# Expert outputs summed in PSUM by group of experts, with gathered residual rows and scattered output rows

## Chip, core and metric

The kernel runs on one core of one Trainium2 chip. The metric is the device time of one execution in microseconds. Time before: median 813.35 us of three runs (811.8 to 814.05).

## What is computed

One encoder layer of 512 tokens with 1024 features: latent attention and pooling, cross attention, a hierarchical mixture of experts, a last norm. The change touches the last two. The group router picks one of 4 groups for each token, then 2 of the group's 8 experts:

```python
group_prob = softmax(xn @ w_rg + b_rg)            # 4 groups
g_w, g_idx = top_k(group_prob, 1)
e_logits = (xn @ w_re + b_re).reshape(B, S, 4, 8)
sel = e_logits of the chosen group
e_w, e_idx = top_k(softmax(sel), 2); e_w = e_w / sum(e_w)
cw[token, expert] = g_w * e_w
out = 0
for e in range(32):
    hid = silu(xn @ w_gate[e]) * (xn @ w_up[e])   # 1024 -> 256
    out = out + (hid * cw[..., e:e+1]) @ w_down[e]
h = h + out
return rms_norm(h, final_norm_g)
```

Both experts of a token lie in one group, so all that the mixture adds to a token comes from 8 consecutive experts.

## The kernel before

Up to `finish_dense` the dense layers run; their instructions are the same in both kernels except for a few small tables of the router. `finish_dense` transposes the residual stream to rows, writes the rows with their 1/rms to the DRAM scratch H3 (512 x 1025) and calls `router`. `router` gives each expert 64 slots and makes `src`, the token of each slot. An empty slot's index is out of bounds, so that its row isn't moved.

`experts` takes the 32 experts as 16 pairs of two, side by side in the columns of TensorE's array. Each expert has three pieces of weights of 1 MB: two of gate and up, one of down. `e_load` issues them on SP's queue in the order of use, into 18 slots of 1 MB (and two places that are used once), so that 20 of the 96 pieces come ahead of the loop; `e_done` hands a slot back when the last product that reads its piece has been issued. The last pair's two pieces of down come in eight quarters. For a pair p the loop does: `up(p)`, 16 products over 8 feature tiles (L1492), then silu on ScalarE (L1502) and the product with up on VectorE (L1503), and the gather of the rows of pair p+3 (L1456, GpSimd); `take(p+1)`, 8 transposes of the next pair's gathered rows (L1474); `turn(p)`, 2 transposes of the hidden rows (L1522); `down(p)`, 8 products (L1538), whose result is scaled by the slot's weight `cws` and split in two float32r halves Y, high by ScalarE (L229) and low by VectorE (L230).

`add(p, i, n)` brings the pair's rows back to the order of the tokens: the one-hot table OH (slots x 512 tokens, by GpSimd in `places`, L1516) times the two halves of Y (L1554), for token tile i and half n of the features, so 8 times two products for each pair, and VectorE adds each bank onto the residual stream in SBUF (L1556). The 8 are queued in `steps`: four run inside the next pair's `up`, one after every second feature tile, two before `turn`, two after it.

The slots' weights `cws` come by memory: `weights` computes two per token, SP writes them to the DRAM scratch CW (L1573), and GpSimd gathers one column for each pair (`weights_of`, L1462). After the last pair, `run` works off the list TAIL: the last adds, squares (L1641), 1/rms (L1644 to L1651), scaling (L1659) and 8 output DMAs of 256 KB (L1661).

Of the kernel before, what the change touches and what calls it, by code (L numbers as in the profile page):

```python
# [6 lines left out]
F32 = mybir.dt.float32  # L7
# [16 lines left out]
# columns of the stacked gains  # L24
# [30 lines left out]
class Arena:  # L55
# [6 lines left out]
    def alloc(self, n, long=False):  # L62
        """the next place after the last one, or for a long time at the top of a gap"""
# [24 lines left out]
    def take(self, at, n):  # L88
        self.used.append((at, at + n))
        self.used.sort()  # L90
        self.peak = max(self.peak, sum(b - a for a, b in self.used))
# [16 lines left out]
class Buf:  # L108
    """A piece of an arena: `ap` is [128, n]; `f` reads it as float32."""
# [33 lines left out]
class Kernel:  # L143
# [8 lines left out]
    TAIL = "a00 p01 | q00 a01 q01 a10 q10 p11 a11 s00 q11 a20 s01 q20 p21 s11 a21 a30 q21 p31 q30 a31 q31 s10 s20 s21 s30 s31"  # L152
    ACT_SCALE = ()
# [60 lines left out]
    # ---- small things  # L214
# [3 lines left out]
    def split(self, src, dst, scale=None, hi_eng="act"):  # L218
        """dst.hi = round(src*scale), dst.lo = src*scale - dst.hi; APs."""
# [23 lines left out]
    # ---- the stream of the dense weights  # L243
# [27 lines left out]
    def w_need(self, upto, ahead=0):  # L271
        """split the weights of the stream up to and with item `upto`, and some more if there is room"""
# [48 lines left out]
    def bcast(self, col, nt, dst):  # L321
        """dst[p, t] = col of token t, for all p"""
# [7 lines left out]
    # =====================================================================  # L330
# [14 lines left out]
    def start(self):  # L345
        nc, a = self.nc, self.a
        # loads
# [22 lines left out]
        # while the first loads come  # L370
# [6 lines left out]
        # constants  # L377
        jp = self.jp = self.const([128, 128], I32, "jp")
        nc.gpsimd.iota(jp, pattern=[[1, 128]], base=0, channel_multiplier=-1)
        self.ident = self.const([128, 128], F32, "ident")  # L380
        nc.vector.tensor_scalar(self.ident, jp, 0.0, None, op0=ALU.is_equal)
        self.ones = {}
# [11 lines left out]
        # x * g in two parts; sums of squares; the first five output tiles  # L394
# [43 lines left out]
        # rotary tables: rows of 32: cos, +-sin, cos, +-sin  # L438
# [11 lines left out]
        # the rotary key, the first pool channels  # L450
# [8 lines left out]
        # latents: kv (2 tiles) and q (3 tiles), raw times their gains, in two parts, and squares  # L459
# [18 lines left out]
        # r1 along the tokens  # L478
# [6 lines left out]
        for n, sc in (("kv", 1.0), ("q", 96.0)):  # L485
# [4 lines left out]
            # (m r1^2 + eps)^-1/2 * r1 (* 1/sqrt(96))  # L490
# [10 lines left out]
        # rotate: rows cos-part, sin-part, twice  # L501
# [32 lines left out]
    def pool_u(self, g, b=None):  # L534
        """pool channels: u, trailing means by doubling"""
# [33 lines left out]
    def mid(self):  # L569
# [18 lines left out]
        # pooled channels  # L588
# [22 lines left out]
        # c_kv along the tokens  # L611
# [9 lines left out]
    def keys(self, j, b):  # L621
        """two heads: rows nope | rope | rope and rope | rope | nope"""
# [10 lines left out]
    def key_rows(self):  # L633
        """the rotary rows are the same for all heads"""
# [7 lines left out]
    def values(self):  # L642
        """values: [keys, head, hi 64 | lo 64]"""
# [25 lines left out]
    # ---- chunk-causal attention, head by head; the first gate's tiles fill the tensor engine  # L669
    def attention(self):  # L670
# [134 lines left out]
        # the last head; the first tiles of the projection of the others  # L805
# [30 lines left out]
    def mix(self):  # L836
        nc, a = self.nc, self.a
        atk = self.atk
        # the residual stream again
# [113 lines left out]
    def cross(self):  # L953
# [3 lines left out]
        # keys [dim, mem]  # L957
# [31 lines left out]
        # values [mem, dim]; the first queries before the last of them  # L989
# [20 lines left out]
        # queries' rstd / sqrt(256)  # L1010
# [93 lines left out]
    # ---- the last projection, the router's logits, the rows for the experts  # L1104
    def finish_dense(self):
# [5 lines left out]
        # rows of the scratch: the residual stream and, in the last column, rstd  # L1111
# [9 lines left out]
        # router weights, hi | lo  # L1121
# [3 lines left out]
        # the last tile's logits come from its float32 rows: the gain goes into the weights  # L1125
# [68 lines left out]
        # (mean of squares + eps)**-0.5: the last tile's part comes alone  # L1194
# [19 lines left out]
        # the logits as rows  # L1214
# [15 lines left out]
    def tmp(self, shape, name, dt=F32):  # L1230
        """a small tile of the arena, freed by tmp_free"""
# [10 lines left out]
    def router_consts(self):  # L1242
# [6 lines left out]
        i32([128, 8], "itile", [[1, 8]], -8, 0)  # L1249
        i32([128, 1], "ipart", [[0, 1]], 0, 1)  # L1250
        self.tri = self.tmp([128, 128], "tri", BF16)
# [3 lines left out]
        # two identities on top of each other: the sum of the parts of the logits  # L1255
# [5 lines left out]
        self.rhs = [self.tmp([128, 4, 3, NE], f"rhs{k}", BF16) for k in range(2)]  # L1261

    def router(self, b):
# [11 lines left out]
        # the group: first maximum; the logits of the experts come meanwhile  # L1275
# [18 lines left out]
        # its experts: the first two maxima, with the others' logits out of reach  # L1294
# [9 lines left out]
        for k in range(2):  # L1304
            nc.vector.tensor_tensor(out=A[k], in0=self.iota64[:, None, :NE].to_broadcast([128, 4, NE]),
                                    in1=I8[:, :, k:k + 1].to_broadcast([128, 4, NE]), op=ALU.is_equal)
            # what the slots shall know of their tokens: its place in the tile, the tile and choice, the tile
            nc.scalar.activation(self.rhs[k][:, :, 0], A[k], AF.Copy, scale=self.ipart)

        def tiles(k, eng):  # L1310
            for v, o in ((1, 4 * k), (2, 4)):
                eng.tensor_tensor(out=self.rhs[k][:, :, v], in0=A[k],
                                  in1=self.itile[:, o:o + 4, None].to_broadcast([128, 4, NE]), op=ALU.mult)
# [15 lines left out]
        # while the ranks come  # L1329
# [6 lines left out]
        self.put(b)  # L1336
# [5 lines left out]
        b = self.bank()  # L1342
        z = self.banks[b][:, :48]
# [5 lines left out]
        z = z.rearrange("p (q e) -> p q e", q=3)  # L1349
# [3 lines left out]
        self.dst = self.const([128, 16], I32, "dst")  # L1353
        nc.vector.tensor_scalar(t1, z[:, 0], 512.0, None, op0=ALU.add)
        nc.vector.scalar_tensor_tensor(out=self.src, in0=z[:, 2], scalar=128.0, in1=t1, op0=ALU.mult, op1=ALU.add)
        nc.vector.tensor_scalar(t1, t1, 512.0, None, op0=ALU.add)
        nc.vector.scalar_tensor_tensor(out=self.dst, in0=z[:, 1], scalar=128.0, in1=t1, op0=ALU.mult, op1=ALU.add)
        self.put(b)
        # the fullest expert
        self.over = self.const([128, 1], I32, "over")  # L1360
        nc.vector.tensor_reduce(out=self.over, in_=cnt, op=ALU.max, axis=AX.X)
        self.put(b2)
        # weights: p(group) / (1 + exp(l2 - l1)) and the rest of it
        w = self.cw = [self.const([128, 4], F32, f"w{k}") for k in range(2)]
        d = c([128, 4], "d21")

        def weights():
            nc.vector.tensor_tensor(out=ge, in0=lg, in1=gm[:, :, None].to_broadcast([128, 4, 4]), op=ALU.subtract)
# [486 lines left out]
```

## Time and profile before

| | |
|---|---|
| median of the runs shown | 813.35 us |
| the profiled execution: span of its trace | 810.7 us |
| its own time outside the trace | not given; the median lies 2.65 us over the span |
| TensorE busy (matmul) | 769.2 us, 95% |
| VectorE, ScalarE, GpSimd busy | 455.1, 303.6, 166.2 us |
| moved by DMA | 157.66 MB |
| TensorE busy, 560 to 780 us | all of it |

The span ends with the last instruction of the slowest engine. A busy TensorE in these pages is a modelled end of each product; the distance between the starts of products is the safer clock. In the rows "idle before <-releaser" names what ended a wait. SPq is SP's queue of DMA issues.

### The profile page before, as it was taken

The numbers are of one execution on the slowest core, as the hardware profiler recorded it, in microseconds if no ns is written. First come the engines' busy times: TensorE is split into PE (matmuls) and PEld (weight loads), VectorE is DVE, ScalarE is ACT, GpSimd is POOL, SyncE is SP. The second block draws the span as 40 slices with busy tenths as digits, with TensorE's granted clock in tenths as the row PEclk, the third lists the DMA queues.
The fourth block names the chain that finished last, engine by engine and source line by source line (L and its number), as shares of the span: only waits on it lengthen the run. The fifth ranks groups of instructions, "written<-read, shape, count | busy, mean of one in ns | idle before, by whom it ended". The sixth has DMA issues, their size and how long they took to land.

```text
span 810.7 us, 10122 instructions
## 1 busy us (share of the span) xinstructions
PE 769.2 (95%) x3714; PEld 522.8 (64%) x3714; DVE 455.1 (56%) x812; ACT 303.6 (37%) x572; POOL 166.2 (21%) x196
## 2 busy tenths in 40 slices
PE   8999999999999989999999998469999999999995
PEld 6877788878786868999888886223344334433342
DVE  6847444777786848874555545114455444544454
ACT  7443323665565625543443443111122211221123
POOL 4245101021111424300001012135312111212002
PEclk9999999999999989999999999599999999999998
DMA  9311323202220733475511999988999999999103
GB/s 329 106 59 29 115 86 123 82 17 72 66 65 27 230 107 85 142 193 153 189 53 29 384 300 278 188 207 323 388 393 401 394 395 387 404 394 412 67 1 106
DMA packets 44868, 157.66 MB, mean 194 GB/s; under 512 B 7568, under 2 KB 17424, under 8 KB 33296
## 3 DMA queue, kind: packets, MB, share of 16 engines
q1 hardware_dynamic: 40992, 149.33, 53.9%
q0 software_dynamic: 3104, 6.31, 2.1%
q10 hardware_dynamic: 720, 1.35, 0.5%
q8 instruction: 30, 0.49, 0.3%
q14 instruction: 22, 0.18, 0.1%
HBM read 156.97 MB, written 4.20 MB: 199 GB/s over the span
## 4 chain that ended last, share of the span: by engine, by line
PE 78%; DVE 6%; DMA 5%; issue 5%; ACT 3%; POOL 3%; SPq 0%; POOLq 0%; DVEq 0%; ACTq 0%
PE b L235 14%; PE b L1492 14%; PE b L236 13%; PE b L237 13%; PE b L1554 8%; PE b L1538 7%; PE b L1474 2%; DMA CW<-w 1%; DMA R<-in_we 1%; PE b L700 1%; PE b L745 1%; DMA F<-in_wd 1%; PE b L702 1%; DVE R L227 1%; PE b L701 1%
## 5 line engine op out<-in xcount | busy, mean ns | idle before, releaser
L1556 DVE TENSOR_TENSOR F<-b,F 128x512 f32<-128x512 f32 x124 | 81.3, 686 | 98.0 <-PE b L1554 98.0
L1554 PE MATMUL b<-B 128*128 128x512 f32 x248 | 81.9, 433 | 5.4 <-ACT B L229 5.4
L1554 PEld LDWEIGHTS b<-B 128*128 128x128 f32 x248 | 40.0, 189 | 58.8 <-issue 49.3
L1502 ACT ACTIVATE F<-b,F 128x256 f32<-128x256 f32 x16 | 7.6, 474 | 135.8 <-PE b L1492 126.1
L1456 POOL DMA_INDIRECT F<-H,src x16 | 17.1, 1066 | 157.6 <-DVE F L1503 143.8
L230 DVE SCALAR_TENSOR_TENSOR B<-b,cws,B 128x512 fp32r<-128x512 f32 x32 | 23.9, 750 | 41.7 <-ACT B L229 41.7
L229 ACT ACTIVATE B<-b,cws 128x512 fp32r<-128x512 f32 x32 | 21.9, 687 | 62.7 <-PE b L1538 52.0
L237 PE MATMUL b<-H,R 128*128 128x512 f32 x108 | 42.8, 397 | 0.0
L1492 PE MATMUL b<-W,F 128*64 128x512 f32 x80 | 38.4, 602 | 0.0
L411 PE MATMUL b<-H,Q 128*128 128x512 f32 x120 | 27.8, 392 | 1.4 <-ACT Q L224 1.4
L1474 PE MATMUL b<-ident,F 128*128 128x128 f32 x128 | 17.6, 283 | 10.5 <-DMA F<-H,src 10.5
L720 ACT ACTIVATE F<-b,sm,cc_q 128x128 f32<-128x128 f32 (+3 forms) x32 | 19.8, 618 | 19.0 <-DVE sm L719 17.4
L411 PEld LDWEIGHTS b<-H,Q 128*128 128x128 f32 x120 | 22.4, 188 | 6.9 <-ACT Q L224 2.3
L235 PE MATMUL b<-H,G 128*128 128x512 f32 x60 | 25.0, 417 | 1.3 <-ACT H L224 1.3
L227 DVE TENSOR_TENSOR R<-W,R 128x1024 fp32r<-128x1024 f32 (+2 forms) x17 | 22.8, 1345 | 5.5 <-ACT R L224 4.8
L1516 POOL TENSOR_SCALAR B<-F,srcf 128x512 fp32r<-128x512 f32 x16 | 25.3, 1586 | 0.5
L1474 PEld LDWEIGHTS b<-ident,F 128*128 128x128 f32 x128 | 15.5, 146 | 14.1 <-DMA F<-H,src 11.4
L236 PE MATMUL b<-H,G 128*128 128x512 f32 x60 | 23.7, 394 | 0.7 <-DVE H L227 0.7
L237 PEld LDWEIGHTS b<-H,R 128*128 128x128 f32 x108 | 20.6, 190 | 4.5
L224 ACT ACTIVATE E<-W 128x1024 fp32r<-128x1024 f32 (+3 forms) x24 | 18.9, 797 | 10.9 <-PE b L236 3.6
L1538 PE MATMUL b<-H,F 128*64 128x512 f32 x96 | 21.9, 599 | 0.8 <-ACT F L1525 0.8
L1479 ACT ACTIVATE F<-b,gcol 128x128 f32<-128x128 f32 x60 | 17.1, 368 | 14.1 <-PE b L1474 14.1
(574 smaller groups left out, 2141.0 us busy)
## 6 DMA issues: line engine op xcount, KB each, us to landing
W<-in_wd SPq DMA_DIRECT2D x62, 512.0 KB, 3.7
H<-in_we SPq DMA_DIRECT2D x20, 1024.0 KB, 8.4
F<-in_we SPq DMA_DIRECT2D x13, 1024.0 KB, 9.9
Q<-in_we SPq DMA_DIRECT2D x12, 1024.0 KB, 7.7
R<-in_we SPq DMA_DIRECT2D x12, 1024.0 KB, 7.6
W<-in_we SPq DMA_DIRECT2D x10, 1024.0 KB, 8.4
E<-in_we SPq DMA_DIRECT2D x5, 1024.0 KB, 8.7
G<-in_we SPq DMA_DIRECT2D x5, 1024.0 KB, 7.8
```

The costliest lines, as they stand in the source:

```text
L227: nc.vector.tensor_tensor(out=lo, in0=src, in1=hi.bitcast(F32), op=ALU.subtract)
L230: nc.vector.scalar_tensor_tensor(out=lo, in0=src, scalar=scale, in1=hi.bitcast(F32), op0=ALU.mult, op1=ALU.subtract)
L235: nc.tensor.matmul(out, l[0], r[0], start=start, stop=False)
L236: nc.tensor.matmul(out, l[0], r[1], start=False, stop=False)
L237: nc.tensor.matmul(out, l[1], r[0], start=False, stop=stop)
L411: nc.tensor.matmul(self.banks[banks[m]], w[l], x[r], start=k == 0 and l + r == 0, stop=k == 7 and l == 1)
L1474: nc.tensor.transpose(self.banks[b][:, k * 128:(k + 1) * 128], x[:, f:f + 128], self.ident)
L1492: nc.tensor.matmul(self.banks[b][r], x[:, k, r], self.e_get(e, k // 4).ap[:, s], start=k == 0, stop=k == 7)
L1516: nc.gpsimd.tensor_scalar(OH[p].ap, self.iotat.ap, self.srcf[:, p:p + 1], None, op0=ALU.is_equal)
L1538: nc.tensor.matmul(self.banks[b][r], h.ap[:, k * 128 + 64 * i:k * 128 + 64 * i + 64], self.e_get(e, 2).ap[:, s], start=k == 0, stop=k == 1)
L1554: nc.tensor.matmul(self.banks[b], OH[p].ap[:, i * 128:(i + 1) * 128], y.ap[:, ns], start=j == 0, stop=j == 1)
L1556: nc.vector.tensor_add(h, self.banks[b].rearrange("p (m f) -> p m f", m=4), h)
```

## The change

- `add` goes by groups. The 4 pairs of a group write into 4 banks (2 tiles of 128 group slots x 2 halves of the features) that stay open over the 4 pairs; 4 times two products for each pair instead of 8 times two, and no add on VectorE. The one-hot table has 256 columns (a token's rank in its group) in place of 512. The adds leave `up`: half of them stand before `turn`, half behind it.
- After a group's last pair, `sums` (VectorE adds of the 4 banks to the residual rows HG, squares on ScalarE), `output` (scaling, and two indirect DMAs on GpSimd that scatter the rows to `out`). `residual` gathers the group's rows of H3 into HG by two indirect DMAs. For the last group the residual goes into the banks by products with the identity, and scaling reads the banks.
- `weights` runs ahead of `take(0)` and is longer. `lists`, behind `up(0)`, makes the slots' ranks and weights (`zs`) and the group's tokens (`gsrc`) by 24 small products. CW, its two writes and the 16 gathers of weights are gone.

```diff
-            for v, o in ((1, 4 * k), (2, 4)):
-                eng.tensor_tensor(out=self.rhs[k][:, :, v], in0=A[k], ...
+            eng.tensor_tensor(out=self.rhs[k][:, :, 1], in0=A[k],
+                              in1=self.itile[:, :, None].to_broadcast([128, 4, NE]), op=ALU.mult)
...
         def weights():
+            for k in range(2):
+                nc.gpsimd.tensor_copy(cb[:, k, :, 0], v)
...
+            nc.vector.tensor_copy(cb[:, :, :, 1], w)
+            for k in range(2):
+                nc.vector.tensor_tensor(out=rhs2[k], in0=A[k][:, :, None, :].to_broadcast([128, 4, 4, NE]),
+                                        in1=cb[:, k, :, :, None].to_broadcast([128, 4, 4, NE]), op=ALU.mult)
+            nc.vector.tensor_tensor(out=JG, in0=self.iotag[:, None, :].to_broadcast([128, 4, 256]),
+                                    in1=v[:, :, None].to_broadcast([128, 4, 256]), op=ALU.is_equal)
+        def lists():
+            for par in range(2):
+                for n in range(8):
+                    nc.tensor.matmul(z[64 * par:64 * par + 64], J[k][:, i], rhs2[k][:, i, :, par::2], ...)
+            nc.scalar.activation(zs, z.rearrange("p (q e) -> p q e", q=4), AF.Copy)
+            for t in range(2):
+                for i in range(4):
+                    nc.tensor.matmul(z[:, 8 * t:8 * t + 8], JG[:, i, t * 128:(t + 1) * 128], rhs3[:, i], ...)
...
-                if k % 2:
-                    step(1)
...
-        def add(p, i, n):
-            b = self.bank()
-                nc.tensor.matmul(self.banks[b], OH[p].ap[:, i * 128:(i + 1) * 128], y.ap[:, ns], start=j == 0, stop=j == 1)
-            nc.vector.tensor_add(h, self.banks[b].rearrange("p (m f) -> p m f", m=4), h)
+        def add(p, n):
+            for t in range(2):
+                if p % PG == 0:
+                    acc[t, n] = self.bank()
+                for j, y in enumerate((Y[p].hi, Y[p].lo)):
+                    nc.tensor.matmul(self.banks[acc[t, n]], OH[p].ap[:, t * 128:(t + 1) * 128], y.ap[:, n * 512:(n + 1) * 512],
+                                     start=p % PG == 0 and j == 0, stop=p % PG == PG - 1 and j == 1)
...
-        weights_of(0)
...
+            if p:
+                add(p - 1, 0)
             turn(p)
-            step(2)
-            if p < NP - 1:
-                down(p)
-                steps += [lambda i=i, n=n, p=p: add(p, i, n) for n in range(2) for i in range(4)]
+            if p:
+                add(p - 1, 1)
+            if p and p % PG == 0:
+                sums()
...
+            down(p)
+            if p and p % PG == 0:
+                output(p // PG - 1)
+            if p % PG == 1:
+                residual(p // PG)
```

TensorE's order from one pair's `up` to the next. Before, with L1492 the products of `up`, L1554 those of `add`, L1474 and L1522 the transposes, L1538 `down`:

```order
L1492 MATMUL b_84<-H,F 64x512 x4
L1554 MATMUL b_83<-B 128x512 x2
L1492 MATMUL b_84<-H,F 64x512 x4
L1554 MATMUL b_78<-B 128x512 x2
L1492 MATMUL b_84<-Q,F 64x512 x4
L1554 MATMUL b_81<-B 128x512 x2
L1492 MATMUL b_84<-Q,F 64x512 x4
L1554 MATMUL b_85<-B 128x512 x2
L1474 MATMUL b_82<-ident,F 128x128 x4
L1474 MATMUL b_80<-ident,F 128x128 x4
L1554 MATMUL b_79<-B 128x512 x2
L1554 MATMUL b_83<-B 128x512 x2
```

Of the changed kernel the same stretch with the rest of the pair (L1540 `up`, L1522 and L1564 the transposes, L1598 `add`, L1580 `down` of the pair):

```order
L1540 MATMUL b_80<-H,F 64x512 x8
L1540 MATMUL b_80<-Q,F 64x512 x8
L1522 MATMUL b_83<-ident,F 128x128 x4
L1522 MATMUL b_82<-ident,F 128x128 x4
L1598 MATMUL b_78<-B 128x512 x2
L1598 MATMUL b_84<-B 128x512 x2
L1564 MATMUL b_79<-ident,F 128x128 x2
L1598 MATMUL b_81<-B 128x512 x2
L1598 MATMUL b_85<-B 128x512 x2
```

The four interruptions of `up` are gone; the adds around `turn` stay as many as they were.

VectorE's order at the start of the experts. Before, `take(0)` (L1481) comes first and the weights (L1368 to L1375) behind it:

```order
L1361 TENSOR_REDUCE over<-b_84 128x1
L1481 TENSOR_SCALAR B<-b_80,gcol 128x128 x4
L1368 TENSOR_TENSOR F<-F 128x16
L1369 TENSOR_TENSOR F<-F 128x4
L1372 TENSOR_REDUCE F<-F 128x4
```

In the changed kernel (L1394 to L1404 are the end of `weights`, L1529 is `take(0)`):

```order
L1394 CAST F<-w 128x8
L1395 TENSOR_TENSOR F<-w,F 128x8
L1396 CAST F<-F 128x8
L1397 TENSOR_TENSOR F<-F 128x8
L1399 TENSOR_TENSOR B<-A_3762,F 128x512
L1399 TENSOR_TENSOR B<-A_3763,F 128x512
L1401 TENSOR_TENSOR B<-iotag,F 128x1024
L1403 TENSOR_SCALAR F<-F 128x4x4
L1404 SCALAR_TENSOR_TENSOR F<-F 128x4x4
L1529 TENSOR_SCALAR B<-b_80,gcol 128x128 x4
```

The two L1399 wait for GpSimd's copies (`cb`), which stand on GpSimd behind the first gathers and two loads; `take(0)` now stands behind all of it.

## Rows read from the trace of the kernel before

**Rows 1.** The page: span, and the span in 40 slices of 20.3 us.

```profile
span 810.7 us, 10122 instructions
...
PE   8999999999999989999999998469999999999995
...
PEclk9999999999999989999999999599999999999998
DMA  9311323202220733475511999988999999999103
```

**Rows 2.** Timeline of TensorE over one pair: start, length, line, tiles, count; the trace counts each float32 product twice.

```profile
645.22 1.89 PE L1492 MATMUL b<-H,F 128*64 128x512 f32 x8
647.03 0.74 PE L1554 MATMUL b<-B 128*128 128x512 f32 x2
...
649.56 0.73 PE L1554 MATMUL b<-B 128*128 128x512 f32 x2
...
654.62 0.73 PE L1554 MATMUL b<-B 128*128 128x512 f32 x2
...
655.98 1.18 PE L1554 MATMUL b<-B 128*128 128x512 f32 x4
...
657.13 1.17 PE L1554 MATMUL b<-B 128*128 128x512 f32 x4
658.23 0.64 PE L1538 MATMUL b<-Q,F 128*64 128x512 f32 x1
...
661.71 0.59 PE L1492 MATMUL b<-G,F 128*64 128x512 f32 x1
```

**Rows 3.** Waits of SP's queue from 540 us on: who waited for whom, us in total, times, longest.

```profile
SPq L1427 <- PE b L1492: 98.0, 24, 11.1
SPq L1427 <- PE b L1538: 74.2, 14, 6.4
```

**Rows 4.** DMA in one pair's time, 644.79 to 661.30 us: packets; then queue, packets, MB, share of the 16 engines (q0 is GpSimd's gathers).

```profile
DMA packets 1012, 6.58 MB, mean 398 GB/s; under 512 B 181, under 2 KB 181, under 8 KB 239
...
q1 hardware_dynamic: 870, 6.32, 95.0%
q0 software_dynamic: 141, 0.24, 3.8%
```

**Rows 5.** Windows: length, busy time of PE, PEld, DVE, ACT, POOL, then granted clock, DMA share, GB/s.

```profile
540.00:560.00 20.00, 14.62 (x56) 6.05 (x56) 7.09 (x14) 3.26 (x8) 13.40 (x12) 0.83 0.91 357
683.00:723.00 40.00, 40.00 (x183) 16.87 (x182) 19.16 (x37) 7.96 (x20) 5.62 (x5) 1.00 0.99 394
723.00:752.00 29.00, 29.00 (x129) 11.27 (x129) 14.00 (x26) 5.53 (x13) 8.16 (x6) 1.00 1.02 411
760.00:780.00 20.00, 20.00 (x92) 7.87 (x88) 9.78 (x18) 4.06 (x9) 0.00 (x0) 1.00 0.00 0
```

**Rows 6.** Timeline of the start of the experts, several engines, in brackets the wait and its releaser.

```profile
506.06 0.74 DVE L1340 TENSOR_TENSOR F<-F 128x256 bf16<-128x256 f32 x2
...
521.17 0.58 POOL L1427 DMA_DIRECT2D C<-in_we  x1
...
522.33 1.97 PE L1474 MATMUL b<-ident,F 128*128 128x128 f32 x8 [10.46 <-DMA F<-H,src]
523.56 1.12 DVE L1481 TENSOR_SCALAR B<-b,gcol 128x128 f32<-128x128 f32 x4 [15.05 <-PE b L1474]
...
506.52 0.97 PE L1347 MATMUL b<-F 128*64 128x48 bf16 x16 [1.23 <-DVE F L1340]
...
534.93 3.65 PE L1538 MATMUL b<-H,F 128*64 128x512 f32 x16 [0.83 <-ACT F L1525]
...
538.61 1.08 POOL L1462 DMA_INDIRECT cws<-CW,dst  x1 [13.12 <-DMA CW<-w]
...
545.68 1.49 PE L1554 MATMUL b<-B 128*128 128x512 f32 x2 [5.38 <-ACT B L229]
```

**Rows 7.** The chain of work that ended last: the piece on the writes of CW (start, us, what).

```profile
526.95 10.88 DMA CW<-w
```

**Rows 8.** The end: timelines of single engines, then the time from issue to landing of the gathers of rows and of the output DMAs.

```profile
789.82 3.65 PE L1538 MATMUL b<-H,F 128*64 128x512 f32 x16
...
793.55 0.69 ACT L229 ACTIVATE B<-b,cws 128x512 fp32r<-128x512 f32 x1 [1.03 <-PE b L1538]
...
793.97 1.02 PE L1626 MATMUL b<-F,ident 128*128 128x512 f32 x2
...
794.78 0.74 DVE L230 SCALAR_TENSOR_TENSOR B<-b,cws,B 128x512 fp32r<-128x512 f32 x1
...
798.00 0.58 ACT L1641 ACTIVATE F<-b 128x512 f32<-128x512 f32 x1
...
803.21 0.27 POOL L1647 TENSOR_SCALAR ms<-ss,ms 128x1 f32<-128x1 f32 x1
803.56 0.55 POOL L1651 TENSOR_TENSOR rs<-ms,expo 128x1 f32<-128x1 f32 x1
...
804.81 0.75 DVE L1659 SCALAR_TENSOR_TENSOR F<-b,rs,F 128x512 f32<-128x512 f32 x1
...
DMA to landing us min/median/max: 4.3/8.4/9.5
...
DMA to landing us min/median/max: 2.3/2.5/3.4
```

More of the change, by code (lines that the diff above doesn't have):

```diff
@@ L1526, in turn, with down @@
             self.put(b)
[L1528 removed]
+        def down(p, between=lambda n: None):
             es = (2 * p, 2 * p + 1)
@@ new lines, in experts, with residual, rows, square @@
+        ms, rs = self.const([128, 2], F32, "ms"), self.const([128, 2], F32, "rs")
+        def residual(g):
+            for t in range(2):
+                nc.gpsimd.indirect_dma_start(
+                    out=HG[t].ap[:, :1025], out_offset=None, in_=self.H3,
+                    in_offset=bass.IndirectOffsetOnAxis(ap=self.gsrc[:, t, g:g + 1], axis=0),
+                    bounds_check=511, oob_is_err=False)
+        def rows(t, n):
+            return HG[t].ap[:, n * 512:(n + 1) * 512]
+        def square(t, n, src):
+            nc.scalar.activation(junk.ap, src, AF.Square, accum_out=ss[n][:, t:t + 1])
+            c = slice(t, t + 1)
+            nc.gpsimd.tensor_scalar(ms[:, c], ss[n][:, c], 1.0 / D, ms[:, c] if n else EPS, op0=ALU.mult, op1=ALU.add)
+            if n:
+                nc.gpsimd.tensor_tensor(out=rs[:, c], in0=ms[:, c], in1=self.expo[:, :1], op=ALU.pow)
@@ L1561, in experts, with sums, output @@
+        def sums():
+            for t in range(2):
+                for n in range(2):
+                    b = acc.pop((t, n))
+                    nc.vector.tensor_add(rows(t, n), self.banks[b], rows(t, n))
+                    self.put(b)
+                    square(t, n, rows(t, n))
+        def output(g):
+            for t in range(2):
+                for n in range(2):
+                    scale(t, n, rows(t, n))
+                scatter(g, t)
         self.e_slots(self.WA)
@@ L1592, in experts @@
                 self.BA = self.seg("B", F32R)
-                XS[0] = self.F(1024)
+                self.hT.free()
+                at = lambda n, o: Buf(self.FA, n, at=o)
+                XS[0] = at(1024, 0)
+                XS.append(at(1024, 1024))
+                self.gl = at(1024, 2048)
                 self.xg_row()
                 gather(2)
-                places(0)
+                HG = [self.F(1025, long=True) for _ in range(2)]
+                for v in HG:
+                    nc.gpsimd.memset(v.ap, 0.0)
@@ L1624, in preload @@
-        def preload(i, n):
-            b = pre[i, n] = self.bank()
-            nc.tensor.matmul(self.banks[b], self.ident, rows[i, n], start=True, stop=False)
-        def last(i, n):
-            if (i, n) not in pre:
-                add(P, i, n)
-                return
-            b = pre[i, n]
-            for j, y in enumerate((Y[P].hi, Y[P].lo)):
-                nc.tensor.matmul(self.banks[b], OH[P].ap[:, i * 128:(i + 1) * 128], y.ap[:, n * 512:(n + 1) * 512],
-                                 start=False, stop=j == 1)
@@ L1663, in run @@
-        def run(order):
-            for op in order.split():
-                i, n = int(op[1]), int(op[2])
-                if op[0] == "p":
-                    preload(i, n)
-                elif op[0] == "a":
-                    last(i, n)
-                elif op[0] == "q":
-                    square(i, n)
-                    done.add((i, n))
-                    if (i, 1 - n) in done:
-                        rstd(i)
-                else:
-                    scale(i, n)
-        done = set()
@@ L1679, in experts @@
-        first, rest = self.TAIL.split("|")
-        down(P, lambda: run(first))
-        run(rest)
-        for b in pre.values():
+            if p:
+                add(p - 1, 1)
+            if p and p % PG == 0:
+                sums()
+            if p == NP - 1:
+                for n in range(2):
+                    for t in range(2):
+                        nc.tensor.matmul(self.banks[acc[t, n]], self.ident, rows(t, n), start=False, stop=False)
+                break
+            down(p)
@@ L1683, in experts, with last @@
+            if p and p % PG == 0:
+                output(p // PG - 1)
+            if p % PG == 1:
+                residual(p // PG)
+        P = NP - 1
+        def last(n):
+            add(P, n)
+            for t in range(2):
+                square(t, n, self.banks[acc[t, n]])
+        down(P, last)
+        for t in range(2):
+            for n in range(2):
+                scale(t, n, self.banks[acc[t, n]])
+            scatter(3, t)
+        for b in acc.values():
             self.put(b)
-        Y.pop(P).free(), OH.pop(P).free()
```

182 lines of the change are left out of this document (86 added, 96 removed).

## The prediction

> **What bounds the kernel now.** First the page in slices [rows 1]: from the 28th slice on (some 547 us) TensorE is full and so are the DMA engines, at 9 of 10, until the weights are all in; in the last slices TensorE works alone. The experts' stage thus has two limits that lie close together, and the prediction turns on how close. The timeline of one pair shows the first [rows 2]: from one `up` to the next 661.71 - 645.22 = 16.49 us, with no idle time on TensorE. The four adds inside `up` start at 647.03, 649.56, ... 654.62, that is every 2.53 us. Eight products of `up` come between two of them; at the pace of `down`, 16 products in 3.65 us less the last one's tail, some 0.215 us each, these are 1.72 us. So one interruption takes 0.81 us: two products of 0.215 us and 0.38 us for the two changes of shape.
>
> The second limit is in the DMA view of the same pair [rows 4]: 6.58 MB in 16.51 us, the hardware queue at 95.0% and GpSimd's gathers at 3.8% of the engines' time. The engines are busy nearly all of it. SP's queue does wait for slots, 172 us in all [rows 3], so the loads are paced by TensorE, but by a TensorE that is hardly slower than the DMA. The windows give 394 GB/s for 683 to 723 us, and 411 at the end of the loads, where the queue is deepest [rows 5]. After 752 us nothing is loaded (760 to 780: 0 GB/s), and TensorE needs 41 us more to its last `down` at 793.5 [rows 8]: that is the stock of loaded pieces, some 2.5 pairs.
>
> **Part by part. Adds out of `up`:** four interruptions of 0.81 us a pair, 3.24 us; TensorE's pair falls from 16.49 to 13.25 us. The adds around `turn` stay the same in number and place, so the cover of silu and of ScalarE's copy stays. A pair's OH and Y are ready one pair earlier, so no new wait. VectorE loses 8 adds a pair and had idle time already: no effect on the end. GpSimd's `places` halves in width: nothing, it was covered.
>
> **What the loads then allow.** From the end of `down(0)` on, 96 - 22 = 74 pieces are still to come (20 ahead of the loop, 2 after `up(0)`): 74 x 1.049 = 77.6 MB. Gathers of 12 pairs at 0.24 MB [rows 4] add 2.9, the residual rows 512 x 4.1 KB = 2.1, the scattered rows of three groups 1.6 MB: 84.2 MB. At 411 GB/s that is 205 us, 16.6 us a pair's worth with the new traffic, and TensorE wants one in 13.25. The stock covers the difference for a while: at `up(p)` 6p + 2 pieces must be there, and 22 + 0.36 x (13.25 (p - 1) - 2) have come (0.36 pieces a us, the weights' share of 411); these meet at p = 12. From then on TensorE waits for weights, and the loads set the end.
>
> **The start.** Before, TensorE waits 5.38 us at 545.68 for ScalarE [rows 6], which stands behind `places`, and that behind the gather of weights, which waited 13.12 us for CW; the write of CW took 10.88 us [rows 7]. All of it goes. `zs` takes its place: 24 small products behind `up(0)`, by the nearest row (16 in 0.97 us [rows 6]) 1.5 us. `weights` now stands ahead of `take(0)` on VectorE. Most of it lies in a wait that VectorE had anyway (508 to 523.56, [rows 6]), but the last five of its instructions wait for GpSimd's two copies, and these stand behind the load that GpSimd issues until 521.75. With 0.2 to 0.6 us a copy (the small rows L1647 and L1651 of GpSimd, [rows 8]) VectorE goes on at 522.5. By L1340 (256 columns in 0.37 us, [rows 6]) the two 512-column products and the 1024-column comparison take about 0.7, 0.7 and 1.4 us, the two small ones 0.3: `take(0)` starts at 525.6 in place of 523.56. Bounds: 0 (copies early) to 4 us. I take 2. So `down(0)` ends at 534.93 + 3.65 + 2 + 1.5 = 542, and `up(1)` follows at once, where before its adds and rows waited to 545.68. SP no longer issues CW; g_final (0.5 MB) moves there, into time in which the DMA is idle.
>
> **End of the loads.** First bytes 2 us after 542 (the shortest issue to landing is 2.3 us, [rows 8]): 544 + 205 = 749.
>
> **Behind the last load.** The last 2 MB are the quarters of `down(15)`, so the second half of `up(15)` can start 5.1 us before and ends 1.7 us before 749. Then on TensorE, in order: add 0.86 and a change 0.3, `turn` 0.4, add 0.86, 4 identity products (0.43 each by L1626's two in about 0.85, [rows 8]) 1.7, changes 0.7: 4.8 us, which covers silu. `down` 3.5 us. It ends 6.6 us behind the loads, at 755.6.
>
> **The tail.** From the end of `down` in rows [rows 8]: L229 0.1 + 0.69, L230 0.75, products 1.2, two squares with their sums 0.77 each, ms and pow 0.27 + 0.55, two scales 0.7 each behind those of the first tile, which overlap: the last scale ends at 7.2 us, GpSimd's issue of the second scatter takes 1.1. From issue to landing I take the shortest gather, 4.3 us, since the queues are empty then; the bounds are the plain outputs' 2.5 and the gathers' usual 8.4. To the end of the span 2.6 us (810.7 less the last plain landing at 808.1). Together 14 to 18, I take 15 (before: 810.7 - 793.5 = 17.2).
>
> Inside the stage, `sums` and `output` give VectorE 8 instructions of 0.7 us in every fourth pair, less than the 8 adds that each pair had; they stand ahead of L229 and L230 of that pair, whose Y is wanted only 10 us later. GpSimd gets 4 indirect DMAs a group of 1.1 us; behind a scatter that waits for VectorE's scales stands the gather of pair p+3, due two pairs later. Both cost nothing. Four of eight banks stay held; the other four turn over once in six uses, each read long before.
>
> **Sum.** 749 + 6.6 + 15 = 770.6 us of span; the median lay 2.65 over the span: 773.3 us, 40 us less.
>
> **Rivals.** (1) *TensorE keeps the bound.* Then the last `down` ends at 542 + 14 x 13.25 + 6.9 + 5 + 3.5 = 743, and the time is 743 + 15 + 2.65 = 760.5. It needs 84.2 MB by 736, 438 GB/s; the rows show 411 at most. The Trainium skill, "DMA: Bandwidth & Descriptors", Specifications, gives a fabric ceiling of 435 GB/s; by it the loads would end at 738 and this rival would come true, but no window here comes near it under gathers.
>
> (2) *The DMA does no better than its average, or waits lower the clock.* At 394 GB/s the loads end at 758 and the time is 782. Waits have cost clock here: in 540 to 560 us, with the 5.38 us wait, the granted clock was 0.83 [rows 5], and a page slice of 0.5 follows the idle 10.46 us [rows 1, 6]. At half clock (1.2 GHz) the 13 us of TensorE behind the last loads would be 5 to 8 longer: up to 790.
>
> (3) *Slower: the scatters block the DMA.* The two small writes of CW took 10.88 us [rows 7], about 8.5 more than the plain outputs' 2.5 [rows 8], and blocked what came behind. If each of the six scatters inside the stage did that, the loads would end 51 us later and the time be 824. It decides from five such blocks on. Against it: CW was written in elements of 4 bytes, the rows are 4 KB. The same section of the Trainium skill says that writes under 512 B become read-modify-write; the rows here are above that, and no row shows a scatter.
>
> (4) *The interruptions come back as waits* (a bank, a gather, Y not ready), the pair stays at 16.5: then only the start is won, some 3 us, and the time is 810.
>
> **How the numbers follow.** Forecast 0.55 (764 to 780), rival 1 0.12, rival 2 0.24 (780 to 790), rival 3 0.05, rival 4 0.04. The range 760 to 789 holds the forecast, nearly all of rival 2 and half of rival 1. A measurement tells 0.3% from no change, 2.4 us. Faster by more: all but rival 3 and half of rival 4, 0.93; within 0.3% 0.02; slower 0.05.
>
> **What the changed profile would show.** `up` without L1598 in it and a pair of 13.2 to 13.6 us in the first half of the stage; no wait for CW; the DMA share at 1.0 to the end of the loads near 749 and above 405 GB/s; TensorE's first waits for weights at pair 11 to 13, in the last pairs some 3 us each; `down(15)` within 8 us of the last load. Wrong would be: waits for weights much earlier or none, a pair above 14 us, the DMA's rate falling around the scatters, or more than 18 us behind `down(15)`.

## The result and the profile after

The changed kernel takes 774.36 us, the median of five runs (769.86 to 775.68). The kernel before took 812.53 us beside it. The ratio is 0.953, with a 95% interval of 0.950 to 0.957: 38 us or 4.7% faster. The forecast was 773.3 us. One execution of all that are told below, of the kernel with two views, took 924.2 us at a granted clock of 0.744; the numbers leave it out.

The profiled execution took 769.86 us, the lowest of the five, with a span of 768.1. Its dense layers happened to be 4 us shorter: the first gather of rows is issued at 513.98, and at 517.99 in the trace of before. Instructions of the dense part are the same, and the other runs told below have this gather anywhere from 514 to 519.5 us.

The page of the kernel after, its span and slices of 19.2 us (to be read against [rows 1]; GB/s is a line of the same view):

```profile
span 768.1 us, 9751 instructions
...
PE   9999999999999889999999999938999999999892
...
PEclk9999999999999999999999999969999999999997
DMA  9321422321130353366451099897999999999950
GB/s 327 108 74 41 124 86 76 106 56 39 38 111 28 126 175 110 84 181 187 129 195 56 28 363 336 276 148 289 419 418 421 418 418 419 418 417 421 417 201 36
```

From the 29th slice to the 38th the DMA moves 417 to 421 GB/s without a break, and the loads end in the 39th of 40. In [rows 1] they ended early in the 38th, of 20.3 us. The DMA now loads almost as long as TensorE computes.

One pair in the timeline of TensorE (start, length, line, tiles, count; against [rows 2]):

```profile
596.36 1.09 PE L1522 MATMUL b<-ident,F 128*128 128x128 f32 x8
597.21 1.17 PE L1598 MATMUL b<-B 128*128 128x512 f32 x4
598.22 0.38 PE L1564 MATMUL b<-ident,F 128*128 128x128 f32 x2
598.36 1.18 PE L1598 MATMUL b<-B 128*128 128x512 f32 x4
599.47 3.65 PE L1580 MATMUL b<-R,F 128*64 128x512 f32 x16
602.95 0.59 PE L1540 MATMUL b<-R,F 128*64 128x512 f32 x1
...
609.92 1.09 PE L1522 MATMUL b<-ident,F 128*128 128x128 f32 x8
```

A pair takes 609.92 - 596.36 = 13.56 us, where [rows 2] had 16.49. `up` runs from 602.95 to 609.92 without an add in it. The adds (L1598) and the transposes around `turn` (L1522, L1564) are as the order showed them.

The pair keeps this length until TensorE meets the end of its stock of weights. The waits of TensorE from 560 to 745 us (who waited for whom, us, times, longest):

```profile
PE b L1540 <- DMA J<-in_we: 2.4, 1, 2.4
PE b L1540 <- DMA Q<-in_we: 1.0, 1, 1.0
PE b L1540 <- DMA F<-in_we: 0.6, 1, 0.6
```

The timeline puts them at 689.35, 704.93 and 722.09 us, in the second half of `up` of pairs 12, 13 and 14. From one silu to the next it takes 13.55 us through pair 11 (13.74 for the first), and then 15.2, 15.6, 18.9 and 13.6. So the listed waits add up to 4.0 us, but pairs 12 to 14 are 9.0 us longer. The timeline at the first wait, below a second half of `up` without one, shows what the list leaves out:

```profile
606.38 3.60 PE L1540 MATMUL b<-F 128*64 128x512 f32 x16
...
687.70 1.02 PE L1540 MATMUL b<-F 128*64 128x512 f32 x2
689.35 3.65 PE L1540 MATMUL b<-F 128*64 128x512 f32 x14 [0.63 <-DMA F<-in_we]
```

Records of the two experts start side by side, 16 in 3.60 us. Where one expert's piece has landed and the other's has not, two records of the first run alone (1.02 us), and of the 14 behind the wait the last two run alone again, so that 14 take as long as 16. Pair 14 has a short wait in its first half too, which the list of the weight loads has (0.84 us at 716.08), and runs for a while at the lower clock (last section).

The same in windows (length, busy time of PE, PEld, DVE, ACT, POOL, then granted clock, DMA share, GB/s; against [rows 5]):

```profile
540.00:560.00 20.00, 20.00 (x102) 9.20 (x100) 4.54 (x12) 5.39 (x14) 6.04 (x6) 1.00 1.02 421
640.00:680.00 40.00, 40.00 (x197) 17.03 (x197) 13.36 (x28) 12.39 (x32) 11.79 (x16) 1.00 1.02 418
700.00:720.00 20.00, 18.76 (x84) 7.03 (x80) 6.46 (x13) 3.82 (x9) 4.58 (x5) 1.00 1.01 419
720.00:740.00 20.00, 17.91 (x78) 7.28 (x80) 3.02 (x7) 3.38 (x8) 2.75 (x3) 0.91 0.95 382
```

The last packet of weights ends at 742.03 us, where before it ended at 753.25. Then 26 us are left, where it was 57.

SP's queue now waits for something else than in [rows 3]. Its waits from 530 us on:

```profile
SPq L1485 <- PE b L1580: 31.8, 7, 7.3
...
SPq L1485 <- DMA R<-in_we: 21.2, 9, 3.2
```

All lines of the second kind, waits for the landing of a load of weights, add up to 121 us, where the kernel before has 3.4. From 598 us to the last issue at 737 just eight loads of weights are under way, and the next is issued 0.06 us behind a landing. The last eight loads are quarters of pieces, so the eight then hold less, and the rate falls at the end: 382 GB/s from 720 to 740 us.

### The profile page after: what moved, and what is told of

Same layout as the page of the kernel before. It is cut to its first block, busy times and chain, and to the rows that moved or that the text cites. A ratio compares the mean times of both kernels' runs of the same rounds, so it can differ in the third digit from the quotient of the medians.

```text
span 768.1 us, 9751 instructions
## 1 busy us (share of the span) xinstructions
PE 725.7 (94%) x3610; PEld 507.0 (66%) x3610; DVE 392.8 (51%) x721; ACT 309.9 (40%) x589; POOL 160.8 (21%) x211
## 5 line engine op out<-in xcount | busy, mean ns | idle before, releaser
L229 DVE SCALAR_TENSOR_TENSOR B<-b,zs,B 128x512 fp32r<-128x512 f32 x32 | 24.0, 751 | 72.9 <-ACT B L228 72.9
L1549 DVE SCALAR_TENSOR_TENSOR F<-b,F 128x256 f32<-128x256 f32 x16 | 7.7, 484 | 97.0 <-ACT F L1548 97.0
L228 ACT ACTIVATE B<-b,zs 128x512 fp32r<-128x512 f32 x32 | 21.9, 686 | 49.6 <-PE b L1580 47.5
L1598 PE MATMUL b<-B 128*128 128x512 f32 x128 | 37.8, 417 | 2.3 <-ACT B L228 1.8
L1540 PE MATMUL b<-W,F 128*64 128x512 f32 x80 | 35.9, 612 | 0.0
L1522 PEld LDWEIGHTS b<-ident,F 128*128 128x128 f32 x128 | 14.4, 146 | 22.3 <-issue 11.7
L1522 PE MATMUL b<-ident,F 128*128 128x128 f32 x128 | 18.3, 289 | 9.8 <-DMA F<-H,src 9.8
L1598 PEld LDWEIGHTS b<-B 128*128 128x128 f32 x128 | 21.6, 189 | 8.1 <-issue 2.6
L1580 PE MATMUL b<-H,F 128*64 128x512 f32 x96 | 22.1, 599 | 1.3 <-ACT F L1567 1.3
L223 ACT ACTIVATE E<-W 128x1024 fp32r<-128x1024 f32 (+3 forms) x24 | 18.9, 798 | 10.9 <-PE b L235 3.6
L1540 PE MATMUL b<-J,F 128*64 128x512 f32 x40 | 19.7, 640 | 2.4 <-DMA J<-in_we 2.4
L223 ACT ACTIVATE G<-W 128x1024 fp32r<-128x1024 f32 (+3 forms) x20 | 17.6, 882 | 9.1 <-PE b L235 3.6
## 6 DMA issues: line engine op xcount, KB each, us to landing
E<-in_we SPq DMA_DIRECT2D x5, 1024.0 KB, 18.9
G<-in_we SPq DMA_DIRECT2D x5, 1024.0 KB, 19.1
```

The lines of the kernel that those rows point to most:

```text
L223: nc.scalar.activation(hi, src, AF.Copy)
L228: nc.scalar.activation(hi, src, AF.Copy, scale=scale)
L229: nc.vector.scalar_tensor_tensor(out=lo, in0=src, scalar=scale, in1=hi.bitcast(F32), op0=ALU.mult, op1=ALU.subtract)
L1522: nc.tensor.transpose(self.banks[b][:, k * 128:(k + 1) * 128], x[:, f:f + 128], self.ident)
L1540: nc.tensor.matmul(self.banks[b][r], x[:, k, r], self.e_get(e, k // 4).ap[:, s], start=k == 0, stop=k == 7)
L1580: nc.tensor.matmul(self.banks[b][r], h.ap[:, k * 128 + 64 * i:k * 128 + 64 * i + 64], self.e_get(e, 2).ap[:, s], start=k == 0, stop=k == 1)
```

## Experiments

Four groups: where TensorE's time went (adds in `up`, adds on VectorE, lists alone), what paces the stage (fewer bytes, in both kernels), what the end is made of (three edits there), and the changed kernel once more for comparison. Ratios are to the kernel before, timed on the same chip.

**The adds back in `up`, as few as they are now.**

```diff
+                if k % 2 and p:
+                    part(p - 1, k // 4, k // 2 % 2)
...
-            if p:
-                add(p - 1, 0)
             turn(p)
-            if p:
-                add(p - 1, 1)
```

> The changed kernel, with the adds of a pair (still 4 times two products into the open banks) back inside the next pair's up, one behind every second feature tile, and none around turn. If the four interruptions are what the change took away, each costs its 0.8 us again: the pair of 13.55 us grows by 3.2 us, gives back some 2.2 us of adds around turn, and shows the waits for silu that these covered (up to 1.5 us): 14.6 to 16.1 us a pair. As the loads bind less then (9 us of waits for weights go), the time rises by 6 to 25 us, to 780 to 799. Rival: only the halved number of products counts. Then the pair stays at 13.5 and the time at 774.

Measured: 801.8 us, ratio 0.988 (0.986 to 0.990); a pair takes 16.00 us throughout. TensorE's timeline in this kernel:

```profile
607.82 0.73 PE L1603 MATMUL b<-B 128*128 128x512 f32 x2
...
610.35 0.73 PE L1603 MATMUL b<-B 128*128 128x512 f32 x2
...
612.88 0.73 PE L1603 MATMUL b<-B 128*128 128x512 f32 x2
613.45 1.03 PE L1522 MATMUL b<-ident,F 128*128 128x128 f32 x8
614.32 0.38 PE L1566 MATMUL b<-ident,F 128*128 128x128 f32 x2
615.99 3.65 PE L1582 MATMUL b<-R,F 128*64 128x512 f32 x16 [1.29 <-ACT F L1569]
```

The interruptions stand 2.53 us apart, as in [rows 2], so an add between products of `up` again costs 0.81 us. And `down` waits 1.29 us for ScalarE's copy of the transposed hidden rows (13 times in the stage), since no add stands around `turn` any more to cover it. Half the products alone is thus worth only 16.50 - 16.00 = 0.5 us a pair: 8 products of 0.215 us are 1.72, less 1.29 of wait. The other 2.45 us of the pair (16.00 to 13.55) come from where the adds stand. In `up` they cost 3.0 us: three times 0.81, and 0.57 for the fourth, from 612.88 to the transposes at 613.45, since it stands at the end of `up` and no product of `up` follows. Around `turn`, from its first transposes to `down`, it takes 615.99 - 613.45 = 2.54 us without them and 599.47 - 596.36 = 3.11 us with them: there all eight products cost 0.6 us, since they run while silu and the copy are waited for. The fourth case, all sixteen products around `turn`, was not run, so how the gain splits in the other order isn't shown. The result lies 3 us above the upper end of what was expected.

**Eight more adds of 128 x 512 on VectorE for each pair**, as many as the change removed, on a tile that nobody reads:

```diff
+            if 0 < p < NP - 1:
+                for _ in range(4):
+                    nc.vector.tensor_add(extra.ap, extra.ap, extra.ap)
```

(These lines stand twice, ahead of `add(p - 1, 0)` and behind `turn(p)`. One takes 0.69 us, as the adds that were removed.)

> The changed kernel, with 8 idle adds of 128x512 on VectorE in each of the pairs 1 to 14 (a scratch tile onto itself, 4 ahead of the transposes of the hidden rows, 4 behind), about as much VectorE work as the adds onto the residual stream were. Theory: VectorE had room, so 774 within 3 us; at most the 4 adds ahead delay the product of silu and up by part of a microsecond a pair. Rival: the relief of VectorE was part of the gain; then up to 14 x 2.8 us come back, 785 or more.

Measured: 774.5 us, ratio 0.956 (0.953 to 0.959), the changed kernel's own time. VectorE is now busy for 28.27 us of this window, where the changed kernel has 14.17, and the pair is 13.55 us all the same:

```profile
580.00:620.00 40.00, 38.81 (x190) 16.61 (x188) 28.27 (x52) 11.74 (x32) 10.52 (x14) 1.00 1.02 420
```

Only the pair behind a group's sums is 1.4 us longer (5 and 9), since `turn` waits 1.2 us for VectorE's product with up there. At the end it costs nothing: the waits for weights that follow are shorter (0.8 and 1.4 us), and the last weights land 228.9 us behind the first gather, as in the changed kernel (228.1, and 229.2 in a second profile). So VectorE's adds were no part of the gain in the pair; what the two longer pairs cost is hidden here by the loads.

**8 MB of weights less** (the second half of each piece of down of pairs 6 to 13 isn't loaded, so that the products use old values there), in the changed kernel and in the kernel before:

```diff
                 n = 512 if len(items) > 1 else 2048 // len(cuts)
+                if items[0][1] == 2 and 12 <= items[0][0] < 28:
+                    n = 1024
```

> The changed kernel, with only the first half of each down piece loaded for the pairs 6 to 13 (8 MB less; the second half of the slot keeps older weights, so the output of these pairs is another). Theory: the loads bind the last pairs. 8 MB are 20 us of DMA, so all waits for weights at pairs 12 to 14 go (1.7 + 2.0 + 5.3 us in the profile, part of the last by a lower clock): 765, with pairs of 13.55 us to the end. Rival: TensorE binds throughout and the longer last pairs are its clock: 774.

> The kernel before, with the same 8 MB less. Theory: there TensorE set the pace of 16.5 us a pair, so no change, 812 within 2 us, with the stock of loaded pieces larger at the end. Rival: the DMA was already the limit before; then up to 20 us less.

Measured: the changed kernel takes 766.3 us, ratio 0.944 (0.942 to 0.946), 8 us less. The kernel before takes 811.8 us, ratio 1.000 (0.998 to 1.002): no change. Windows of the changed kernel with fewer bytes at the end of its loads:

```profile
700.00:720.00 20.00, 20.00 (x98) 8.12 (x98) 9.46 (x17) 7.84 (x19) 7.19 (x12) 1.00 1.00 413
720.00:740.00 20.00, 20.00 (x98) 8.35 (x95) 3.50 (x8) 3.85 (x9) 3.22 (x4) 1.00 0.34 126
```

TensorE has no waits for weights left and all its pairs last 13.55 us. This is the step from one limit to the other: before, bytes are free and TensorE's pair is what counts; after, bytes count. 8.39 MB at 419 GB/s would be 20 us; after 8 of them TensorE is the limit. 766 us is what the change would have reached if the loads had not bound.

**The slots' weights by on-chip products alone**, in the kernel before (`lists` behind the first `up`, no CW; `weights` stays behind `take(0)`, adds as before):

```diff
-            nc.sync.dma_start(CW.rearrange("(k t p) o -> k p (t o)", k=2, p=128)[k], self.cw[k])
...
-        weights_of(0)
...
             up(p)
             if p == 0:
+                self.lists()
```

> The kernel before with one part of the change alone: the slots' weights come from on-chip products behind the first up, not by way of the DRAM scratch CW. The adds stay per pair, inside the next up. Theory: this part is worth the start alone. The profiled change won 9.5 us between the first two pairs' silus; the pair itself stays at 16.5 us and nothing waits for weights, so the time is 812 - 9.5 = 802 to 803 us. Rival (the wait at the start only moved to a later place, since the loads are close behind): 808 to 812 us.

Measured: 804.5 us, ratio 0.990 (0.988 to 0.993), 7.8 us less. The first two silus lie 15.94 us apart and lay 23.20 before, 7.3 less; every other pair is 16.50. The start in TensorE's timeline:

```profile
536.35 3.65 PE L1555 MATMUL b<-H,F 128*64 128x512 f32 x16 [1.29 <-ACT F L1542]
...
541.65 0.73 PE L1571 MATMUL b<-B 128*128 128x512 f32 x2
```

The add at 541.65 follows without a wait, where [rows 6] had 5.38 us. The interval doesn't hold 1, and no later wait takes the gain back. It is less than the 9.5 us expected, because those held the shorter `up(1)` of the changed kernel as well.

**The end: no products with the identity** (VectorE adds the last group's residual rows, as for the other groups); **both halves of the last `down` ahead of the adds** (`between(n)` holds the adds and squares of half n; with the change the first half's adds stand behind the second half's products, and its squares behind those adds); **both**:

```diff
-                        nc.tensor.matmul(self.banks[acc[t, n]], self.ident, rows(t, n), start=False, stop=False)
...
+                nc.vector.tensor_add(rows(t, n), self.banks[acc[t, n]], rows(t, n))
```

```diff
             for n in range(2):
...
+                if n:
+                    between(0)
                 ns = slice(n * 512, (n + 1) * 512)
...
-                between(n)
+            between(1)
```

> The changed kernel, but the last group's residual rows are added by VectorE at the end, as for the other groups, in place of four identity products per float32 copy on TensorE before the last down. Theory: what lies behind the last load is a chain of TensorE's work, of which these products took 3.60 us; they go, and four adds of 0.7 us come on VectorE, of which about two lie on the chain (the scales read SBUF, not PSUM): a gain of 2 to 2.5 us, 772 us. Rival: the products ran in time in which TensorE waited for the last weights anyway, the adds then only lengthen the end: 775 to 776 us.

> The changed kernel, but in the last pair both halves of down run before the adds of the first half, in place of an add between the halves that TensorE has to wait for. Theory: the two waits of 0.96 and 0.81 us around the last adds go, one becomes shorter at most, and the second half's scaling and split start earlier: a gain of 1 to 2.6 us, 772 to 773 us. Rival: the squares of the first half, which come later now, take the place of what is won: 774 us, no change.

> Both of the two changes at the end together: no identity products, and both halves of the last down before the adds. Theory: the gains add up, since each takes a different piece out of the same chain: 4 to 5 us, 769 to 770 us. Rival: only the larger one counts, 772 us.

Measured: 771.3 us, ratio 0.950 (0.947 to 0.952); 770.7 us, 0.950 (0.947 to 0.952); both 768.8 us, 0.947 (0.945 to 0.950). From the landing of the last weights to the end of the span it is 26.1 us in the changed kernel, 23.9, 23.3 and 22.0 in these three: 2.1 and 2.7 alone, 4.1 together. The pieces add up nearly, as pieces of one chain do. The medians fall by 3.1, 3.7 and 5.5 us, but the first two intervals overlap that of the changed kernel (0.950 to 0.957): for each edit alone the gain is shown for the profiled execution, and only both together are clear of it in time, just. With both halves first, TensorE's end reads:

```profile
750.09 3.65 PE L1580 MATMUL b<-H,F 128*64 128x512 f32 x16
753.67 1.45 PE L1600 MATMUL b<-B 128*128 128x512 f32 x5
755.34 0.96 PE L1600 MATMUL b<-B 128*128 128x512 f32 x3 [0.22 <-DVE B L229]
```

`down` is in one piece, and one wait of 0.22 us is left of two pairs of waits (below).

**The changed kernel again, the same with two disjoint views of the output for the two scatters of a group, and this with both edits at the end:**

```diff
+        views = [v.rearrange("b t d -> (b t) d") for v in dram_disjoint_views(self.out, 2)]
...
-                out=self.out.rearrange("b t d -> (b t) d"), in_=HG[t].ap[:, :1024], in_offset=None,
+                out=views[t], in_=HG[t].ap[:, :1024], in_offset=None,
```

> The changed kernel itself once more, beside the two next ones, so that they can be compared with it under the same conditions. Every theory: 772 to 776 us, as before (774.36).

> The changed kernel, but the two scatters of a group write to the output through two views that are declared disjoint (they are: each row belongs to one token), so that the second need not wait until the first has landed. Theory: the wait of 3.14 us before the last scatter is on the path that sets the end; the second scatter is issued right behind the first, some 1.1 to 1.4 us after it in place of 4.2, and the end comes 2.5 to 3 us sooner: 771 to 772 us. Rival: both go through the same queue, and the second then lands no sooner than before: 774 us, no change.

> All three changes at the end: no identity products, both halves of the last down before the adds, and two disjoint views for the scatters. Theory: they take different pieces out of one chain, so it is 5.5 us (the first two) and 2.5 to 3 us (the views) below the changed kernel: 766 us. Rival: the last weights' landing, which varies by the run, hides a part: 768 to 769 us.

Measured: 773.9 us, ratio 0.955 (0.953 to 0.958); with the views 773.8 us, 0.954 (0.951 to 0.956); all three edits 767.9 us, 0.946 (0.944 to 0.948). GpSimd's timeline of the kernel with the views:

```profile
762.13 1.09 POOL L1632 DMA_INDIRECT out<-F,gsrc  x1 [0.83 <-DVE F L1626]
763.53 0.98 POOL L1632 DMA_INDIRECT out<-F,gsrc  x1 [0.30 <-DVEq L1731]
```

The second scatter follows the first by 1.4 us in place of 4.2, and the span ends 23.4 us behind the last weights in place of 26.1 (19.1 with all three edits). So the trace shows the 2.7 us that were expected, in one execution each; the times do not, since the two intervals overlap. That the views are worth 2.7 us is shown for the profiled execution and open for the median. The version with all three edits beats the changed kernel by 6 us with intervals that don't touch, and has the lowest median of all that were run. It came out at the rival's 768 and not at the 766 us expected, and its interval overlaps that of the version with two edits (0.945 to 0.950), so the views' share is open there too.

## Why the prediction was right

**TensorE's pair: right.** Forecast 13.25 us, or 13.2 to 13.6 in the list of what would show it; measured 13.55. The term that was mis-sized is the fourth interruption. It stands at the end of `up`, and [rows 2] has its start at 654.62. What follows is no product of `up`:

```profile
655.19 1.04 PE L1474 MATMUL b<-ident,F 128*128 128x128 f32 x8
```

That is 0.57 us and not 0.81. `up` with its adds took 655.19 - 645.22 = 9.97 us and takes 6.97 now, so the four were worth 3.00 and not 3.24. The stretch around `turn` stayed nearly as it was, as forecast: 658.23 - 655.19 = 3.04 before, 3.11 now. The reason given, that the place of the adds counts more than their number, is what the adds put back in `up` showed: 2.45 us for the place, 0.5 for the number.

**The loads take the bound from pair 12 on: right.** The first wait for weights comes in pair 12. The loads bind, shown by 8 MB less: 8 us in the changed kernel, none in the kernel before. The rate was forecast as 411 GB/s for 84.2 MB behind `down(0)`. The trace has 412 GB/s as the mean from 537.4 to 742.1 us, which is 84.3 MB: 418 to 421 most of the time, less at the end, so that the mean comes out at 411 is in part luck. (411 was no rate of a deep queue: in that window of the kernel before, some three loads were under way until 740 us.) This is why the gain is 38 us and not 46, the 766 us of the run with fewer bytes.

**The start: right in kind, mis-sized.** The chain over CW is gone. `take(0)` was to come 2 us later and the lists to take 1.5. The timeline of the kernel after, several engines:

```profile
513.98 1.29 POOL L1510 DMA_INDIRECT F<-H,src  x1 [12.62 <-DMA R<-in_we]
...
517.71 0.36 POOL L1389 CAST F<-F 128x4 bf16<-128x4 f32 x2
517.97 1.29 DVE L1399 TENSOR_TENSOR B<-A,F 128x512 bf16<-128x512 f32 x2 [10.58 <-POOL F L1389]
...
520.54 1.12 DVE L1529 TENSOR_SCALAR B<-b,gcol 128x128 f32<-128x128 f32 x4
...
528.36 0.57 PE L1414 MATMUL b<-B,F 128*64 128x64 bf16 x16
...
528.87 0.36 PE L1426 MATMUL b<-F,B 128*128 128x8 bf16 x8
529.08 1.07 PE L1522 MATMUL b<-ident,F 128*128 128x128 f32 x8
...
531.72 3.65 PE L1580 MATMUL b<-H,F 128*64 128x512 f32 x16 [1.35 <-ACT F L1567]
```

VectorE did wait for GpSimd's copies, as forecast, and from the first gather to `take(0)` it is 6.56 us, where [rows 6] and the gather at 517.99 give 5.57: 1.0 in place of 2. The 24 small products hold TensorE for 0.7 us, from 528.36 to the transposes at 529.08, where 1.5 were forecast. `down(0)` ends 21.4 us behind the first gather, 0.8 later than before and not 3.5. The lists alone gave 7.8 us; in the changed kernel the first two silus lie 9.5 us closer than before, of which 3.0 are the shorter `up(1)`, so the start is worth some 6.5 there. The fourth rival, in which only the start is won, put it at 3.

**Behind the last load: the term that was too small.** `down(15)` was to end within 8 us of the last load, and it did not. Forecast 6.6 us to the end of the last `down`, measured 753.25 - 742.03 = 11.2. The timelines of single engines at the end, against [rows 8]:

```profile
740.94 1.20 PE L1598 MATMUL b<-B 128*128 128x512 f32 x4
...
743.31 3.60 PE L1698 MATMUL b<-F,ident 128*128 128x512 f32 x8
746.83 1.94 PE L1580 MATMUL b<-H,F 128*64 128x512 f32 x8
749.72 0.47 PE L1598 MATMUL b<-B 128*128 128x512 f32 x1 [0.96 <-ACT B L228]
750.42 0.96 PE L1598 MATMUL b<-B 128*128 128x512 f32 x3 [0.22 <-DVE B L229]
751.31 1.94 PE L1580 MATMUL b<-H,F 128*64 128x512 f32 x8
...
757.27 2.73 DVE L1625 SCALAR_TENSOR_TENSOR F<-b,rs,F 128x512 f32<-128x512 f32 x4 [2.48 <-POOL rs L1622]
...
758.98 1.10 POOL L1629 DMA_INDIRECT out<-F,gsrc  x1 [0.83 <-DVE F L1625]
763.21 0.97 POOL L1629 DMA_INDIRECT out<-F,gsrc  x1 [3.14 <-DMA out<-F,gsrc]
```

Two sizes were wrong. The four identity products took 3.60 us and not 1.7: L1626's two in 0.85 [rows 8] was read as two products, but two records are one float32 product, as the heading of [rows 2] says of the others. And `down` was taken as one piece of 3.5 us; the adds of its first half stand between the halves and wait 0.96 and 0.22 us, so it takes 6.4. That makes 1.9 + 2.9 = 4.8 us, of which 0.2 came back elsewhere. Taking them away shortened the end by 2.1 and 2.7 us.

**The tail** from there was 14.85 us, forecast 15, though not by its own steps: the second scatter waits 3.14 us for the landing of the first, which the forecast didn't have, and the last two land in 3.0 us (median), sooner than the 4.3 taken. That the sum fits is luck.

**The sum** came out within 1.1 us of the median because errors went both ways, and so close a fit is luck. In the span: 7 us too late at the end of the loads (4 of them the shorter dense part of this execution, the rest the start), 4.6 too early behind them. And the median lies 6.3 us over this span, where 2.65 were added, since the profiled execution was the fastest of its five (its own time is 1.8 over its span).

**The rivals.** TensorE did not keep the bound (1): the run with fewer bytes puts that case at 766, not 760.5. It needed 438 GB/s, and the best of the windows shown has 421. (The 411 of the rows was not the most to be seen before: single slices of 6.8 us of that trace, from 540 us on, reach 424.) Of the second (2), the waits did lower the clock once, with no cost to be seen (below), and the rate was not the 394 of the kernel before. The scatters did not block the DMA (3): windows around them have the same rate as those without, 418 GB/s in 640 to 680 us, where two run. No interruption came back as a wait in the pairs (4).

## What to carry to other kernels

Where two limits lie close together, price a gain on one by the other: find how long the stock of loaded data lasts at the new pace, and what the DMA needs for what is left. Here TensorE could give 46 us and the loads allowed 38. An instruction of another shape in the middle of a long run on TensorE costs more than itself (0.81 us for 0.43 us of products), and the same instruction put where TensorE would wait anyway costs a fraction of itself (eight products for 0.6 us). Once the loads bind, each microsecond of work behind the last load is one of the kernel's, and it is cheap to find there: the order of the last pair and the identity products together gave 5 us.

## What the runs showed of the hardware

- A DMA share of 0.99 was not the DMA's limit. The kernel before moves 394 to 398 GB/s at that share [rows 4, 5], paced by TensorE, as the run with fewer bytes shows; the changed kernel moves 418 to 421 at 1.01 to 1.02. More loads are under way at a time: between 560 and 680 us their median from issue to landing is 21.3 us, and 8.1 before. That this is what raises the rate was not tried; but the changed kernel has 421 GB/s already from 540 to 560 us, with some four loads under way, so eight are not needed for it.
- Two scatters to one output run one after the other unless they write through views that are declared disjoint. GpSimd's waits at the scatters of the changed kernel (us, times), and the time from issue to landing:

```profile
  DMA out<-F,gsrc: 28.0, 4
...
DMA to landing us min/median/max: 2.6/7.7/9.0
```

  In the stage that is 8.1 to 8.4 us for each of three groups, and GpSimd has the time; at the end it was 3.14 us of the path.
- A wait of 2.36 us at 722.09 was followed by a granted clock of 0.57 in the window 723 to 727 us, that is mostly the lower level of 1.2 GHz. The changed kernel's second profile had waits of 0.4, 1.0, 2.03 and 1.17 us and a clock of 1.00 from 720 to 740. The length of the wait alone doesn't decide: a wait of 2.07 us in the kernel without identity products was followed by the lower level too, one of 2.20 in the kernel with the other order was not. Pairs 14 and 15 took 32.4 us together with the lower clock and 32.6 without it: while the weights set the pace, no cost of the clock shows in these two.
